# A decoder trunk on one core: the down weights' sums behind the units' stores, the down product's parts made further ahead and spread

## The chip, the core and the metric

The kernel runs on one core of a Trainium2 chip. The metric is the device time of one execution in microseconds (us), the median of several runs. The engines are named as in the profile: PE is TensorE (matmuls), PEld its weight loads, DVE is VectorE, ACT is ScalarE, POOL is GpSimd and SP is SyncE, which here only issues DMAs. Each engine takes its instructions in the order in which they stand in its own queue. The framework's planner draws up these orders when the kernel is built, from the order of the program, from priorities that the program sets, from the dependences between tiles, and from edges that the program adds.

## The reference

One layer of a decoder on 1024 tokens of width 1024, all in float32. An attention sub-layer with three groups of heads comes first, then the part that matters here, a gated MLP with D_FF = 2816, then a gated embedding and a last norm:

```
r = r + mix @ w_out
h2 = rmsnorm(r, ffn_norm)
gate = causal_dwconv(h2 @ w_gate) + conv_b
r = r + (gelu(gate) * (h2 @ w_up)) @ w_down
gate = sigmoid(rmsnorm(r, ple_norm) @ w_ple_gate)
r = r + (p @ w_ple_proj) * gate
return rmsnorm(r, final_norm)
```

## The kernel before

Every float32 matmul is made of three: each operand is split into a high part, rounded to the matmul's type (ACT, line 770), and a low part, the rest (DVE, line 771), and `mm3` (lines 113 to 117) adds high by high, high by low and low by high in PSUM.

**The output projection** (`out_tile_half`, lines 810 to 819) makes r tile by tile, in 16 halves. Each takes a slice of w_out, loaded by SP and split by ACT (line 102) and DVE (line 104), and a half of the residual's input; the result is also stored to HBM by POOL (`r_dram`, line 818).

**The units.** The MLP's 22 tiles of 128 hidden channels are 22 units. Gate and up product of one unit are computed together by seven products of half size (a Strassen scheme: sums of weights and sums of activations are multiplied instead of the four blocks). A product (`prod`, line 916) is 12 matmuls of 128x512, a unit 84. The products add into three PSUM banks "a", "b" and "d"; between them ACT copies a bank out (line 941) or DVE adds it to a tile (lines 944 and 978), and the product that adds into the same bank next has to wait for that. The order from unit 3 on is 1, 5, 6, 2, 7, 3, 4, with the addition of line 944 between 7 and 4 (while 3 runs). The weights of a unit are prepared one to two units ahead (`weights_up_1`, `weights_up_2`, with a high priority). At its end a unit multiplies by the gate (lines 988 and 989) and POOL stores the result for the down product: an even unit stores `he` (line 992), an odd one `ho`, then the differences with its even partner, `ta` and `tb` (lines 995, 1000 and 1003).

**The sums of the down weights** (`sums_down`, lines 1005 to 1015). The down product is of the same scheme, so it needs sums of the blocks of w_down. They are made in 22 slices: POOL loads four blocks of 128x256 (512 KB, line 1009) into one tile for which there is a single buffer (tag "rs"), DVE makes four additions (lines 1011 and 878), POOL stores the tile to HBM (`s_dram`, line 1015). They depend on no unit. In the program slice n stands before unit n+3, but the planner gives them the place where the engines' queues are free for them: POOL issues the first load at 385.2 us, in the attention's end, and the last at 733.4 us, in the middle of the units.

**The down product** (lines 1062 to 1164) has seven products in the order `DOWN = (1, 2, 6, 5, 7, 3, 4)`, each of 11 steps (one for each pair of units), 77 steps in all. A step is 12 matmuls. Its operands are 512 KB of weights and activations for two steps, loaded from HBM by SP and split by ACT and DVE, a pair of steps at a time (`parts`, lines 1073 to 1089): weights into the buffers "whi" and "wlo" (two each), activations, loaded for four steps, into "big" (16). Raw weights go to "wraw" (one buffer) and "ws" (three), raw activations to "hx" (six). At step 4 all eight tiles of the residual are loaded back (`residual`, line 1097), which fills four of the six "hx" buffers. At the end of a product DVE adds its four banks to the residual (line 1156), and where a quarter of the residual is then complete (`DONE`) the program makes at once, for its four tiles, the squares for the next norm and the high and low part that the gate's matmuls will read (`done`, lines 1105 to 1121). After the products 2, 6 and 5 a slice of the gate's weights is prepared (`gate_weights`).

**The gate and the end** (`embed`, `finish`) follow, 24 groups of 24 matmuls.

Of the kernel before, what the change touches and what calls it, by code (L numbers as in the profile page):

```python
# [73 lines left out]
def trunk(ctx: ExitStack, tc: tile.TileContext, a, out, dbg):  # L74
# [18 lines left out]
    def half(h):  # L93
        return slice(h * H2, (h + 1) * H2)
# [696 lines left out]

    he_dram = [dp.tile([P, H2], F32, name=f"hed{j}") for j in range(NJ)]
    ho_dram = [dp.tile([P, T], F32, name=f"hod{j}") for j in range(NJ)]
    ta_dram = [dp.tile([P, T], F32, name=f"tad{j}") for j in range(NJ)]
    tb_dram = [dp.tile([P, T], F32, name=f"tbd{j}") for j in range(NJ)]
    s_dram = [dp.tile([4, P, H2], F32, name=f"sd{j}") for j in range(NJ)]
    B = {n: [None] * 4 for n in range(1, 8)}
# [111 lines left out]
    class Unit:  # L909
# [21 lines left out]
        def rest(self):  # L931
# [59 lines left out]
            if f % 2 == 0:  # L991
                G.dma_start(he_dram[j], u1)
# [9 lines left out]
            minus(e1, u1, t2)  # L1002
            G.dma_start(tb_dram[j], even[j])

    def sums_down(n):

        j, c = n // 2, slice(n % 2 * 256, n % 2 * 256 + 256)
        t = cp.tile([P, 4, 256], F32, tag="rs", bufs=1, name=f"sd{n}")
        G.dma_start(t, a["w_dn"][j][:, :, c].rearrange("b p c -> p b c"))
        a11, a12, a21, a22 = [t[:, i, :] for i in range(4)]  # L1010
        V.tensor_tensor(out=a22, in0=a21, in1=a22, op=ALU.add)
        minus(a21, a11, a21)
        minus(a11, a22, a11)
        minus(a12, a12, a11)
        G.dma_start(s_dram[j][:, :, c].rearrange("b p c -> p b c"), t)

    even = []
    lft = [t[:, half(0)] for t in r]
# [45 lines left out]

    def operands(i, j):

        w = a["w_dn"][j]
        x = {1: w[0], 2: w[1], 4: w[3], 6: s_dram[j][0], 3: s_dram[j][1], 7: s_dram[j][2], 5: s_dram[j][3]}[i]
        y = {1: he_dram[j], 2: ho_dram[j][:, half(1)], 3: ho_dram[j][:, half(0)], 5: ta_dram[j][:, half(0)],
             6: ta_dram[j][:, half(1)], 7: tb_dram[j][:, half(0)], 4: tb_dram[j][:, half(1)]}[i]  # L1070
        return x, y

    def parts(g):

        with tc.high_priority(offset=300):
            if g % 2 == 0:
                raws[g // 2] = f4("hx", f"hr{g}", (P, 4, H2))
                for x in range(4 * (g // 2), min(len(steps), 4 * (g // 2) + 4)):
                    nc.sync.dma_start(raws[g // 2][:, x % 4, :], operands(*steps[x])[1])
            n = min(2, len(steps) - 2 * g)  # L1080
            rw = f4("ws" if g % 2 else "wraw", f"wdr{g}", (P, 2, H2))
            for x in range(n):
                nc.sync.dma_start(rw[:, x, :], operands(*steps[2 * g + x])[0])
            got = []
            for raw, tags in ((rw, ("whi", "wlo")), (raws[g // 2][:, g % 2 * 2:g % 2 * 2 + 2, :], ("big", "big"))):
                hi, lo = [f4(t, f"{c}{t}d{g}", (P, 2, H2), F32R) for c, t in zip("hl", tags)]
                hl(hi[:, :n], lo[:, :n], raw[:, :n])
                got.append((hi, lo))
        return got
# [15 lines left out]
    def done(d, h):  # L1105

        c = half(h)
        if not acc3:
            acc3.append(f4("ws", "acc3"))
        if d == (0 if h else 4):  # L1110
            S.square(acc3[0][:, c], r[d][:, c])
        else:
            sq = fp.tile([P, H2], F32, tag="s1", bufs=1, name=f"sq{d}{h}")
            S.square(sq, r[d][:, c])
            V.tensor_tensor(out=acc3[0][:, c], in0=acc3[0][:, c], in1=sq, op=ALU.add)
# [4 lines left out]
        V.scalar_tensor_tensor(out=lo[:, c], in0=r[d][:, c], scalar=col(C_G3 + d), in1=hi[:, c].bitcast(F32),  # L1120
                               op0=ALU.mult, op1=ALU.subtract)
# [15 lines left out]
    got = {}  # L1137
    bank = {}
    for n, (i, j) in enumerate(steps):
        if n % 2 == 0:  # L1140
            got[n // 2] = parts(n // 2)
        if n == 4:
            for x in range(4):
                residual(x)
        (wh, wl), (xh, xl) = got[n // 2]
# [7 lines left out]
        if j == NJ - 1:  # L1153
# [147 lines left out]
def layout(x, p, positions, attn_norm, w_in, hgrn_lb, hgrn_gnorm, attn_sinks, w_out, ffn_norm, w_gate, w_up, conv_w,  # L1301
# [15 lines left out]
    }  # L1317
    a["w_dn"] = w_down[0].reshape(NJ, 2, P, 2, H2).transpose(0, 3, 1, 2, 4).reshape(NJ, 4, P, H2)
    a.update(constants())
# [18 lines left out]
```

## Time and profile before

| | us |
|---|---|
| median of 3 runs | 1305.1 |
| lowest and highest | 1305.02, 1309.39 |
| the profiled execution's own time | 1310.03 |
| its span, first to last instruction | 1308.3 |
| output projection and embedding's first product, about | 404 to 531 |
| units | 531 to 972 |
| down product | 972 to 1197 |
| gate, embedding, last norm | 1197 to 1308 |

| engine | busy us | share |
|---|---|---|
| PE | 1249.9 | 96% |
| DVE | 907.7 | 69% |
| ACT | 553.1 | 42% |
| POOL | 128.1 | 10% |

The mean granted clock of TensorE in this execution is 0.982 of full speed. Views of the trace that are used below: the page (shares of each engine), the view by stretches (busy time, instruction counts and clock in given windows), the timeline (instructions of one engine in order, with the idle time before each and what ended it), the view of waits (who waited for whom) and the table of DMA issues (size, and median time from issue to landing). "sd<-w_dn" is a load of a slice of the down weights, "sd<-sd" its store; "wdr", "hr" and "rr" are raw weights, raw activations and the residual of the down product.

### The profile page before, as it was taken

The numbers are of one execution on the slowest core, as the hardware profiler recorded it, in microseconds if no ns is written. First come the engines' busy times: TensorE is split into PE (matmuls) and PEld (weight loads), VectorE is DVE, ScalarE is ACT, GpSimd is POOL, SyncE is SP. The second block draws the span as 40 slices with busy tenths as digits, with TensorE's granted clock in tenths as the row PEclk, the third lists the DMA queues.
The fourth block names the chain that finished last, engine by engine and source line by source line (L and its number), as shares of the span: only waits on it lengthen the run. The fifth ranks groups of instructions, "written<-read, shape, count | busy, mean of one in ns | idle before, by whom it ended". The sixth has DMA issues, their size and how long they took to land. (4 is left out here: it accounts for less than half of the span.)

```text
span 1308.3 us, 16434 instructions
## 1 busy us (share of the span) xinstructions
PE 1249.9 (96%) x6198; PEld 1041.7 (80%) x6198; DVE 907.7 (69%) x1567; ACT 553.1 (42%) x860; POOL 128.1 (10%) x162
## 2 busy tenths in 40 slices
PE   9999999999999789999999999999999899899996
PEld 7888888887888577777777788888887788688896
DVE  7986967566776377988777766776666555565576
ACT  6324233356773143644334343433344433453432
POOL 2000000021112223011112100000000000000010
PEclk9999999999999889999999999999999899899998
DMA  6110011111017746354555423332568555443132
GB/s 245 49 33 24 26 33 33 33 33 33 17 49 256 252 159 217 113 166 172 185 191 184 153 77 105 121 110 94 167 238 295 182 190 170 135 161 116 41 106 81
DMA packets 62414, 165.04 MB, mean 126 GB/s; under 512 B 7488, under 2 KB 10048, under 8 KB 62336
## 3 DMA queue, kind: packets, MB, share of 16 engines
q1 hardware_dynamic: 45136, 106.45, 24.7%
q0 software_dynamic: 15616, 55.84, 12.0%
q10 hardware_dynamic: 1584, 1.71, 0.4%
q8 instruction: 48, 0.79, 0.2%
q14 instruction: 30, 0.25, 0.1%
HBM read 119.67 MB, written 44.30 MB: 125 GB/s over the span
## 5 line engine op out<-in xcount | busy, mean ns | idle before, releaser
L115 PE MATMUL d<-hbigd,hwhid 128*128 128x512 f32 x308 | 122.2, 398 | 6.8 <-ACT hwhid L770 4.2
L116 PE MATMUL d<-lbigd,hwhid 128*128 128x512 f32 x308 | 122.1, 397 | 1.2 <-DVE lbigd L771 1.2
L117 PE MATMUL d<-hbigd,lwlod 128*128 128x512 f32 x308 | 121.8, 395 | 0.7 <-DVE lwlod L771 0.7
L771 DVE TENSOR_TENSOR lwlod<-wdr,hwhid 128x1024 fp32r<-128x1024 f32 (+1 forms) x39 | 47.0, 1208 | 70.8 <-ACT hwhid L770 70.7
L770 ACT CAST hwhid<-wdr 128x1024 fp32r<-128x1024 f32 (+1 forms) x39 | 40.4, 1039 | 99.6 <-PE d L116 98.0
L115 PE MATMUL gb<-b,hf 128*128 128x512 f32 x176 | 70.2, 399 | 6.5 <-DVE us L944 4.8
L115 PEld LDWEIGHTS d<-hbigd,hwhid 128*128 128x128 f32 x308 | 59.0, 192 | 20.5 <-ACT hwhid L770 5.0
L115 PE MATMUL gd<-b,f 128*128 128x512 f32 x176 | 68.9, 392 | 3.5 <-ACT us L941 3.4
L116 PEld LDWEIGHTS d<-lbigd,hwhid 128*128 128x128 f32 x308 | 59.1, 192 | 14.2 <-DVE lbigd L771 1.9
L117 PEld LDWEIGHTS d<-hbigd,lwlod 128*128 128x128 f32 x308 | 59.1, 192 | 13.7 <-DVE lwlod L771 1.5
L117 PE MATMUL gd<-b,f 128*128 128x512 f32 x176 | 68.3, 390 | 1.5 <-DVE f L771 1.5
L116 PE MATMUL gb<-b,hf 128*128 128x512 f32 x176 | 69.3, 394 | 0.0
L117 PE MATMUL gb<-b,lf 128*128 128x512 f32 x176 | 69.3, 394 | 0.0
L116 PE MATMUL gd<-b,f 128*128 128x512 f32 x176 | 68.5, 389 | 0.0
L115 PE MATMUL pg<-hp,hpg 128*128 128x256 f32 (+1 forms) x192 | 61.7, 321 | 0.0
L116 PE MATMUL pg<-lp,hpg 128*128 128x256 f32 (+1 forms) x192 | 61.3, 319 | 0.0
L117 PE MATMUL pg<-hp,lpg 128*128 128x256 f32 (+1 forms) x192 | 61.1, 318 | 0.0
L771 DVE TENSOR_TENSOR lbigd<-hr,hbigd 128x1024 fp32r<-128x1024 f32 (+1 forms) x39 | 46.9, 1206 | 11.7 <-ACT hbigd L770 11.4
L770 ACT CAST f<-wg 128x512 fp32r<-128x512 f32 x22 | 13.7, 624 | 80.2 <-PE gd L117 80.2
L115 PEld LDWEIGHTS gb<-b,hf 128*128 128x128 f32 x176 | 33.3, 189 | 17.9 <-DVE us L944 6.9
L770 ACT CAST hbigd<-hr 128x1024 fp32r<-128x1024 f32 (+1 forms) x39 | 40.3, 1038 | 16.3 <-DMA hr<-hod 8.9
L771 DVE TENSOR_TENSOR f<-s,f 128x1024 fp32r<-128x1024 f32 x22 | 26.9, 1222 | 28.0 <-ACT f L770 27.8
(459 smaller groups left out, 3513.1 us busy)
## 6 DMA issues: line engine op xcount, KB each, us to landing
sd<-w_dn POOLq DMA_DIRECT2D x22, 512.0 KB, 4.3
sd<-sd POOLq DMA_DIRECT2D x22, 512.0 KB, 3.8
wu<-w_gu SPq DMA_DIRECT2D x22, 512.0 KB, 3.5
wg<-w_gu SPq DMA_DIRECT2D x22, 512.0 KB, 3.6
wdr<-sd SPq DMA_DIRECT2D x44, 256.0 KB, 3.0
wdr<-w_dn SPq DMA_DIRECT2D x33, 256.0 KB, 3.0
wr_wo<-w_out SPq DMA_DIRECT2D x16, 512.0 KB, 4.0
hod<-us POOLq DMA_DIRECT2D x11, 512.0 KB, 3.1
```

Of the source, the lines that this page charges most:

```text
L115: TE.matmul(o, wh, xh, start=first, stop=False, skip_group_check=on)
L116: TE.matmul(o, wh, xl, start=False, stop=False, skip_group_check=on)
L117: TE.matmul(o, wl, xh, start=False, stop=last, skip_group_check=on)
L770: S.copy(hi, src)
L771: e.tensor_tensor(out=lo, in0=src, in1=hi.bitcast(F32), op=ALU.subtract)
```

## The change

1. `sums_down(n)` queues its load behind the last store of unit n+2 (unit 21 for the last three) with an edge in POOL's queue (`issue_after`). Each unit notes its last store in `sent`. In an odd unit the `ho` store moves behind the `ta` store.
2. The buffers in HBM for `he`, `ho`, `ta`, `tb` and the sums become one tensor each over all pairs, with w_down laid out to match, so that the loads of up to four steps become one DMA (`load_steps`).
3. The down product's weights are split into "r" buffers (eight, which is four pairs of steps) from pair 2 to pair 32, and into "whi" and "wlo" or "big" before and after; raw weights rotate over "wraw" and two turns of "ws".
4. The residual's tiles are loaded at the steps 4, 6, 12 and 15, two tiles each, instead of all at step 4.
5. `done` is no longer called for four tiles at once: the calls go to a list, and one is taken at every odd j (the step within a product), from step 56 on at every step. For the first four tiles the parts are made once at full width, when the second half is complete.

```diff
-    he_dram = [dp.tile([P, H2], F32, name=f"hed{j}") for j in range(NJ)]
...
-    s_dram = [dp.tile([4, P, H2], F32, name=f"sd{j}") for j in range(NJ)]
+    he_dram = dp.tile([NJ, P, H2], F32, name="hed")
+    ho_dram, ta_dram, tb_dram = [dp.tile([NJ, P, T], F32, name=n) for n in ("hod", "tad", "tbd")]
+    s_dram = dp.tile([4, NJ, P, H2], F32, name="sd")
...
-                G.dma_start(he_dram[j], u1)
+                sent[f] = G.dma_start(he_dram[j], u1)
...
-            G.dma_start(ho_dram[j], us)
...
             G.dma_start(ta_dram[j], cv)
...
-            G.dma_start(tb_dram[j], even[j])
+            G.dma_start(ho_dram[j], us)
+            sent[f] = G.dma_start(tb_dram[j], even[j])
...
-        G.dma_start(t, a["w_dn"][j][:, :, c].rearrange("b p c -> p b c"))
+        with tc.issue_after(sent[min(n + 2, NF - 1)].ins):
+            G.dma_start(t, a["w_dn"][:, j, :, c].rearrange("b p c -> p b c"))
...
+    def load_steps(t, x0, n, which):
+
+        x = x0
+        while x < x0 + n:
+            i, j = steps[x]
+            m = min(x0 + n - x, NJ - j)
+            nc.sync.dma_start(t[:, x - x0:x - x0 + m, :], OPERANDS[i][which][j:j + m].rearrange("j p t -> p j t"))
+            x += m
+
+    LAST = 6 * NJ // 2
...
-                for x in range(4 * (g // 2), min(len(steps), 4 * (g // 2) + 4)):
-                    nc.sync.dma_start(raws[g // 2][:, x % 4, :], operands(*steps[x])[1])
+                load_steps(raws[g // 2], 2 * g, min(4, len(steps) - 2 * g), 1)
             n = min(2, len(steps) - 2 * g)
-            rw = f4("ws" if g % 2 else "wraw", f"wdr{g}", (P, 2, H2))
-            for x in range(n):
-                nc.sync.dma_start(rw[:, x, :], operands(*steps[2 * g + x])[0])
+            rw = f4(("wraw", "ws", "ws")[g % 3], f"wdr{g}", (P, 2, H2))
+            load_steps(rw, 2 * g, n, 0)
+            tags = ("whi", "wlo") if g < 2 or g >= LAST and (g - LAST) % 3 else ("r", "r") if g < LAST else ("big", "big")
...
+        if d < 4:
+            if h:
+                return
+            c = slice(0, T)
...
+    todo = []
     for n, (i, j) in enumerate(steps):
         if n % 2 == 0:
             got[n // 2] = parts(n // 2)
-        if n == 4:
-            for x in range(4):
-                residual(x)
+        if n in (4, 6, 12, 15):
+            residual((4, 6, 12, 15).index(n))
+        if n > 5 * NJ and todo or todo and j % 2:
+            done(*todo.pop(0))
...
             if i in DONE:
-                d0, h = DONE[i]
-                for d in range(4):
-                    done(d0 + d, h)
+                todo += [(DONE[i][0] + d, DONE[i][1]) for d in range(4)]
...
+    for x in todo:
+        done(*x)
```

More of the change, by code (lines that the diff above doesn't have):

```diff
@@ L1014, in sums_down @@
         minus(a12, a12, a11)
-        G.dma_start(s_dram[j][:, :, c].rearrange("b p c -> p b c"), t)
-    even = []
+        G.dma_start(s_dram[:, j, :, c].rearrange("b p c -> p b c"), t)
+    even, sent = [], {}
     lft = [t[:, half(0)] for t in r]
@@ L1063, in trunk @@
     raws = {}
[L1065 to L1071, printed above, removed]
+    wd = a["w_dn"]
+    OPERANDS = {1: (wd[0], he_dram), 2: (wd[1], ho_dram[:, :, half(1)]), 4: (wd[3], tb_dram[:, :, half(1)]),
+                6: (s_dram[0], ta_dram[:, :, half(1)]), 3: (s_dram[1], ho_dram[:, :, half(0)]),
+                7: (s_dram[2], tb_dram[:, :, half(0)]), 5: (s_dram[3], ta_dram[:, :, half(0)])}
+    def load_steps(t, x0, n, which):
[6 more added lines that the diff above has]
+    LAST = 6 * NJ // 2
     def parts(g):
@@ L1077, in parts @@
                 raws[g // 2] = f4("hx", f"hr{g}", (P, 4, H2))
[L1078 to L1079 removed]
+                load_steps(raws[g // 2], 2 * g, min(4, len(steps) - 2 * g), 1)
             n = min(2, len(steps) - 2 * g)
[L1081 to L1083 removed]
+            rw = f4(("wraw", "ws", "ws")[g % 3], f"wdr{g}", (P, 2, H2))
+            load_steps(rw, 2 * g, n, 0)
+            tags = ("whi", "wlo") if g < 2 or g >= LAST and (g - LAST) % 3 else ("r", "r") if g < LAST else ("big", "big")
             got = []
[L1085 to L1086 removed]
+            for raw, ts in ((rw, tags), (raws[g // 2][:, g % 2 * 2:g % 2 * 2 + 2, :], ("big", "big"))):
+                hi, lo = [f4(t, f"{c}{'wh'[len(got)]}d{g}", (P, 2, H2), F32R) for c, t in zip("hl", ts)]
                 hl(hi[:, :n], lo[:, :n], raw[:, :n])
@@ L1317, in layout @@
     }
-    a["w_dn"] = w_down[0].reshape(NJ, 2, P, 2, H2).transpose(0, 3, 1, 2, 4).reshape(NJ, 4, P, H2)
+    a["w_dn"] = w_down[0].reshape(NJ, 2, P, 2, H2).transpose(3, 1, 0, 2, 4).reshape(4, NJ, P, H2)
     a.update(constants())
```

3 lines of the change are left out of this document (removed).

## The prediction

> **What bounds the kernel now.** The page comes first, for the engine that the span hangs on.
>
> ```profile
> span 1308.3 us, 16434 instructions
> PE 1249.9 (96%) x6198; PEld 1041.7 (80%) x6198; DVE 907.7 (69%) x1567; ACT 553.1 (42%) x860; POOL 128.1 (10%) x162
> ```
>
> TensorE (PE) is busy 96% of the span. What can be won without taking matmuls away is PE's idle time, and time at a lowered clock. The view by stretches shows where these lie: its columns are the stretch, its length, the busy time and instruction count of PE, PEld, DVE, ACT and POOL, the granted clock, the DMA engines' busy share and GB/s.
>
> ```profile
> 404.00:424.00 20.00, 18.76 (x82) 14.91 (x81) 9.88 (x14) 6.52 (x8) 6.57 (x9) 1.00 0.98 350
> 424.00:446.00 22.00, 15.53 (x56) 12.24 (x55) 6.17 (x10) 4.35 (x6) 6.98 (x8) 0.77 0.80 273
> 446.00:456.00 10.00, 8.33 (x38) 6.55 (x37) 4.87 (x8) 2.25 (x4) 2.53 (x4) 1.00 0.60 197
> 456.00:476.00 20.00, 15.35 (x66) 12.64 (x65) 12.45 (x31) 5.11 (x7) 4.81 (x7) 0.83 0.69 223
> ...
> 531.00:572.00 41.00, 36.49 (x156) 28.54 (x155) 36.80 (x56) 21.14 (x30) 2.23 (x3) 1.00 0.37 125
> 572.00:745.00 173.00, 162.93 (x696) 130.45 (x695) 137.59 (x201) 66.43 (x80) 28.22 (x42) 0.99 0.51 174
> 745.00:965.00 220.00, 219.96 (x971) 181.88 (x970) 152.48 (x188) 87.06 (x105) 12.90 (x24) 1.00 0.34 115
> ...
> 985.00:995.00 10.00, 8.76 (x38) 6.63 (x37) 6.41 (x6) 6.00 (x6) 0.00 (x0) 1.00 0.83 276
> ...
> 1030.00:1046.00 16.00, 12.35 (x43) 9.40 (x42) 11.36 (x15) 7.59 (x11) 0.00 (x0) 0.79 0.50 165
> ...
> 1130.00:1146.00 16.00, 12.15 (x42) 9.01 (x41) 12.45 (x16) 9.37 (x14) 0.00 (x0) 0.79 0.47 154
> ```
>
> The stretch 745:965 is undisturbed: 971 matmuls in 220 us, 0.2266 us each. With that as the price of one, a stretch loses its length less its count times 0.2266. (Counts include matmuls that straddle an end, and a few of 128 columns, so this is good to some 0.3 us.) In the order of the rows: 20 - 82 x 0.2266 = 1.4; 9.3; 1.4; 5.0; 5.7; 15.3; nothing; 1.4; 6.3; 6.5. So 17.1 us go in the output projection (404 to 476), 21.0 in the first half of the units (531 to 745) and 14.2 in the down product. These 52 us are what the change can reach. The second half of the units runs without loss, with the same code.
>
> What differs between the halves of the units is the sums of the down weights. The timeline of DVE shows what they do to it, in the projection and in the units; the bracket is the idle time before an instruction and what ended it.
>
> ```profile
> 435.31 0.42 DVE L1011 TENSOR_TENSOR sd<-sd 128x256 f32<-128x256 f32 x1 [10.02 <-DMA sd<-w_dn]
> ...
> 451.07 0.43 DVE L1011 TENSOR_TENSOR sd<-sd 128x256 f32<-128x256 f32 x1 [5.22 <-DMA sd<-w_dn]
> ...
> 464.56 0.43 DVE L1011 TENSOR_TENSOR sd<-sd 128x256 f32<-128x256 f32 x1 [5.60 <-DMA sd<-w_dn]
> ...
> 737.35 0.42 DVE L1011 TENSOR_TENSOR sd<-sd 128x256 f32<-128x256 f32 x1 [2.81 <-DMA sd<-w_dn]
> ...
> 738.30 0.68 DVE L944 TENSOR_TENSOR us<-gb,us 128x512 f32<-128x512 f32 x1
> ```
>
> DVE takes its instructions in order. At L1011, the first sum of a slice, it stands still until the slice has landed, and all that is queued behind it stands as well: the weights' low parts at L104 in the projection, in the units L944, which empties the bank that PE's next product adds to. The timeline of PE answers within 2 us:
>
> ```profile
> 436.92 0.80 PE L117 MATMUL o<-ha,wl_wo 128*128 128x512 f32 x1 [6.47 <-DVE wl_wo L104]
> ...
> 739.04 0.50 PE L115 MATMUL gb<-b,hf 128*128 128x512 f32 x1 [1.91 <-DVE us L944]
> ...
> 1037.77 0.79 PE L115 MATMUL d<-hbigd,hwhid 128*128 128x512 f32 x1 [3.65 <-ACT hwhid L770]
> ...
> 1136.09 1.22 PE L115 MATMUL d<-hbigd,hwhid 128*128 128x512 f32 x2 [2.66 <-ACT hbigd L770]
> ```
>
> The last two are the down product's own stalls. The DVE rows just before the second show the cause: the residual's additions (L1156) and the gate's parts and squares (L1120, L1115) come in one bunch after a product's last step, and the next steps' weights and operands (L771) stand among and behind them.
>
> ```profile
> 1130.44 1.88 DVE L1156 TENSOR_TENSOR rr<-d,rr 128x512 f32<-128x512 f32 x3
> 1132.24 0.74 DVE L1120 SCALAR_TENSOR_TENSOR lp<-rr,small,hp 128x512 fp32r<-128x512 f32 x1
> 1132.90 0.68 DVE L1115 TENSOR_TENSOR acc<-acc,sq 128x512 f32<-128x512 f32 x1
> 1133.50 1.41 DVE L1120 SCALAR_TENSOR_TENSOR lp<-rr,small,hp 128x512 fp32r<-128x512 f32 x2
> 1134.83 1.22 DVE L771 TENSOR_TENSOR lwlod<-wdr,hwhid 128x1024 fp32r<-128x1024 f32 x1
> ```
>
> **The sums leave the projection.** Nothing is removed: 22 loads and 22 stores on POOL's queue and 88 additions on DVE remain, at 0.42 us about 37 us of DVE. They move. The edge puts load n behind the last store of unit n+2, so no sum can start before unit 2 is done, three units of 19 us (84 matmuls) after 531. In the projection the three long blocks of DVE go, and with them 9.3 + 1.4 + 5.0 = 15.7 us of PE. What is late next are the loads of w_out and of the residual: with the DMA engines 98% busy the stretch from 404 lost 1.4 us, so I leave as much standing and take 14.3. Bounds: 5, if these loads take over two thirds of it, and 16.5, if the sums' traffic was also what made them late.
>
> **The sums in the units.** 13 of them lie in 531 to 745 now, at a loss of 15.3 us from 572 on: 1.2 us per sum. The 5.7 us before 572 belong to the first units (the operands' parts, and a weight load on which ACT waits) and stay. After the change 19 sums lie in the units, one to each of 19, always at the same place in the unit. Whether that place is harmless I work out in an undisturbed unit.
>
> ```profile
> 751.17 0.53 POOL L1003 DMA_DIRECT2D tbd<-us  x1 [0.41 <-DVE us L878]
> ...
> 768.50 0.55 POOL L992 DMA_DIRECT2D hed<-us  x1 [16.80 <-DVE us L989]
> ```
>
> ```profile
> 752.94 1.22 DVE L771 TENSOR_TENSOR f<-s,f 128x1024 fp32r<-128x1024 f32 x1 [2.07 <-ACT f L770]
> ...
> 757.30 0.68 DVE L944 TENSOR_TENSOR us<-gb,us 128x512 f32<-128x512 f32 x1
> ```
>
> ```profile
> 759.82 0.39 PE L115 MATMUL gb<-b,hf 128*128 128x512 f32 x1
> ```
>
> ```profile
> sd<-w_dn POOLq DMA_DIRECT2D x22, 512.0 KB, 4.3
> ...
> wdr<-sd SPq DMA_DIRECT2D x44, 256.0 KB, 3.0
> ...
> hr<-hod SPq DMA_DIRECT2D x22, 256.0 KB, 5.6
> ...
> rr<-rd SPq DMA_DIRECT2D x8, 512.0 KB, 7.1
> ```
>
> After an odd unit the load is issued at 751.7, when the tbd store has left POOL, and lands 4.3 us later, at 756.0. The matmul that needs L944 starts at 759.82. If the planner puts L1011 right behind the low part of 752.94, DVE waits from 754.2 to 756.0, then has 1.7 us of sums and, up to the end of L944, 3.2 us of its own work: 760.9, so PE waits 1.1 us. If it stands two instructions later, it delays nothing that PE waits for: L944 ends at 757.98 + 1.7 = 759.7. After an even unit the load is issued at 769.05 and lands at 773.35, and the same sum (4.9 us) gives 778.3; PE's matmul is due 84 matmuls after 759.82, at 778.86: no wait. With half of the 1.1 us in 9 odd units that is 5 us; the loss of 15.3 becomes 5, a gain of 10.3. Bounds: 0 per sum (gain 15.3), or the 1.2 per sum of now, 22.8 in all (7.5 worse than now). DVE has room: it was idle 67 of the 220 us from 745 on, and 19 sums put 32 us there and before.
>
> Moving the ho store behind the ta store delays it by about 2 us (it waits for the second subtraction); who waits is ACT's next copy into a "us" buffer at L941, needed by PE's product 3, which begins some 3 us later. POOL's queue has nothing else behind these loads. I cost it at nothing; if the cover is gone, it is at most 1 us in an odd unit.
>
> **The down product.** The gate's parts of a row tile come one or two steps apart, and the weights' parts are made into "r" buffers, four pairs ahead where "whi" and "wlo" allow two. A pair is 24 matmuls, 5.4 us, so the lead grows from 11 to 22 us, and the bunch, four tiles of 0.6 + 0.7 + 0.7 us on DVE, is under 10. The stalls of 6.3 and 6.5 us go; for the four tiles whose parts are now made at full width from step 66 on I leave 0.8 us: gain 12.0, between 8 and 12.8. The larger loads (up to four steps in one) move the same bytes with fewer issues on SP; they cost nothing while the lead holds.
>
> What gets worse is the start of the product. The last three sums stand behind unit 21's last store, which now leaves POOL at about 980, one after another through one buffer. There the DMA engines are 83 to 100% busy, the residual tiles take 7.1 us to land, and the lead is only what was made before 972. A load in such company blocked DVE for 10.02 us at 425. On the other side the residual's four loads are spread over twelve steps, and the weights' lead fills faster. From 0 to 10 us more than the 1.4 of now; I take 2, near the lower end, since the pairs' parts go before the sums in the planner's order. The stores' buffers in HBM become one each for he, ho, ta, tb and the sums. Should a load now wait for all stores to its buffer, the sums' last store (980 plus three rounds of 13 us, the 173 us of the stretch over its 13 sums: 1019) still lies ahead of step 22, at 1030. The rest, from 1197 on, is not touched.
>
> **Sum.** 14.3 + 10.3 + 12.0 - 2 = 34.6 us. The profiled execution took 1310.0 us (1308.3 and 1.7 around it), which gives 1275.4. The median of the runs shown is 4.9 lower, 1305.1, and I take the gain over to it: 1270.5.
>
> **Rivals.** *The sums cost in every unit what they cost now*, 1.2 us. For it is the row of the view of waits for 572 to 745 (us in total, times, longest), by which six of 13 sums made DVE wait, at no fixed place:
>
> ```profile
> DVE sd L1011 <- DMA sd<-w_dn: 16.3, 6, 4.1
> ```
>
> Against it is the fixed place worked out above. Then 14.3 - 7.5 + 12.0 - 2 = 16.8: 1288. *Loads take over*: PE in the projection and at the start of the product then waits for DMA. For it are the shares of 0.98 and 0.80; against it that they include the sums' own traffic. 5 + 10.3 + 8 - 10 = 13.3: 1292. *The change doesn't do what it says*: the edge binds POOL alone, the planner fills DVE's queue anew, and blocks of the same length arise elsewhere; the projection's 14.3 come back as waits in the units, and in the down product one of two stalls stays (12.0 - 6.3) while its start costs 5: under 1 us, 1304. *Slower*: every sum hits L944 as the one at 737 did. PE waited 1.91 us there and then ran cold, 3.4 us in all (the row below); 19 of these are 65 against 14.3 + 15.3 + 12.0 - 2 = 39.6, so 1305.1 + 25 = 1330. It decides from 2.1 us per sum. Against it: only one of 13 sums did so.
>
> The cold clock is the other part of that price:
>
> ```profile
> 736.00:746.00 10.00, 8.09 (x29) 6.16 (x29) 7.77 (x12) 3.97 (x4) 0.75 (x1) 0.83 0.40 128
> ```
>
> 10 - 29 x 0.2266 = 3.4, though PE waited only 1.91. The Trainium skill (TensorE: Matmul & The Clock Gate, "HAM oscillation — how this bites in real kernels") has the clock fall after idle gaps of more than about 3.4 us. By that rule the slower rival would cost the wait alone, 19 x 1.91 = 36 against 39.6, and would end at 1302. The row disagrees: 1.91 us were enough here, so I keep 1330.
>
> **Chances.** The forecast has 0.68, sums as dear as now 0.13, loads 0.09, no change 0.05, slower 0.05. The range reaches from 1257 (all best bounds give 16.5 + 15.3 + 12.8 = 44.6, 1260.5, and a little for the stall of 5.7 that I left) to 1290, past the first rival, and leaves out the others. About 0.5% (6.5 us) is what a measurement of this kernel can tell from no change. Faster by more: the first three cases but for their tails, 0.88; the same 0.07; slower 0.05.
>
> **What would show it.** Right: no L1011 before the third unit is done; PE at 46 matmuls per 10 us from 415 to 510; 22 units at 19.0 to 19.6 us each; no clock below 1.00 near 1035 and 1140; the first sum of each unit waiting under 2 us. Wrong: L944 or L104 still releasing PE after a wait for sd; PE waits on hbigd or hwhid between 975 and 1030 of over 4 us in all; a unit pitch over 20.

## The result

| | before | after |
|---|---|---|
| median of 4 runs each, us | 1305.06 | 1272.21 |
| lowest and highest | 1303.04, 1309.39 | 1269.89, 1273.43 |
| ratio, with its 95% interval | | 0.9742 (0.9713 to 0.977) |
| the profiled execution, its span | 1310.03, 1308.3 | 1272.79, 1270.8 |

The forecast was 1270.5. The page of the changed kernel shows PE's busy share up by a point on a span 37.5 us shorter:

```profile
span 1270.8 us, 16249 instructions
PE 1236.2 (97%) x6198; PEld 1034.7 (81%) x6198; DVE 903.2 (71%) x1563; ACT 551.7 (43%) x856; POOL 130.2 (10%) x162
```

The view by stretches, with the columns explained in the prediction, for the projection (first four rows), the units (three) and the down product (two):

```profile
404.00:424.00 20.00, 20.00 (x89) 16.38 (x88) 8.52 (x10) 7.74 (x10) 6.75 (x8) 1.00 0.92 322
424.00:446.00 22.00, 22.00 (x103) 18.36 (x102) 9.18 (x12) 6.65 (x9) 5.81 (x7) 1.00 0.77 281
446.00:456.00 10.00, 10.00 (x50) 8.37 (x49) 7.28 (x20) 3.54 (x6) 2.49 (x3) 1.00 0.49 147
456.00:476.00 20.00, 20.00 (x90) 16.58 (x89) 17.22 (x22) 11.35 (x15) 8.35 (x8) 1.00 0.39 127
508.00:549.00 41.00, 35.94 (x149) 28.39 (x148) 33.64 (x49) 19.63 (x29) 0.72 (x1) 0.96 0.29 98
549.00:722.00 173.00, 170.94 (x746) 139.06 (x745) 137.19 (x190) 71.78 (x87) 22.23 (x35) 1.00 0.47 153
722.00:944.00 222.00, 218.57 (x960) 179.36 (x958) 167.97 (x233) 87.83 (x104) 28.87 (x44) 1.00 0.53 174
1015.00:1025.00 10.00, 6.99 (x24) 5.04 (x23) 7.68 (x8) 6.88 (x8) 0.00 (x0) 0.83 0.53 176
1025.00:1159.00 134.00, 134.00 (x593) 110.99 (x592) 75.60 (x79) 56.38 (x64) 1.43 (x2) 1.00 0.53 176
```

PE is busy in all 72 us of the projection that lost 17.1 before, and in all 134 us from 1025 to 1159, at a clock of 1.00. Counted by matmuls, the second old stall stood ahead of the 57th step, which PE now starts at 1102.32, inside these 134 us; the first stood ahead of the 23rd, which it now starts at 1004.07, and there it lost 0.7 us (at 1005.22). Two things are new: a hole of 10 - 24 x 0.2266 = 4.6 us at 1015, and small losses all along the units (549 to 944), whose second half had none before.

From here on a stage's length runs from its first matmul to that of the next stage. What PE lost in it is the time between the starts of two matmuls beyond the price of the first, summed over the timeline of PE.

| stage | before: length, lost | after: length, lost | gain by the loss | forecast |
|---|---|---|---|---|
| projection, 395 to the units | -, 23.6 | -, 0.7 | 22.9 | 14.3 |
| units | 440.6, 21.7 | 435.7, 16.7 | 5.0 | 10.3 |
| down product | 225.0, 15.6 | 215.2, 5.7 | 9.9 | 12.0 - 2 |
| gate and end | 110.9 | 111.3 | -0.4 | 0 |

Three terms, each off by something, add up to 37.4 against a forecast of 34.6; by the medians the gain is 32.9. The profiled execution of before lay 5 us above its median, that of after 0.6, so the table's losses before are those of a long execution.

The timeline of DVE shows where the sums stand now; the bracket is the idle time before an instruction and what ended it:

```profile
664.69 0.42 DVE L1010 TENSOR_TENSOR sd<-sd 128x256 f32<-128x256 f32 x1 [1.75 <-DMA sd<-w_dn]
...
669.10 0.69 DVE L942 TENSOR_TENSOR us<-gb,us 128x512 f32<-128x512 f32 x1
...
840.15 0.68 DVE L942 TENSOR_TENSOR us<-gb,us 128x512 f32<-128x512 f32 x1
...
841.35 0.42 DVE L1010 TENSOR_TENSOR sd<-sd 128x256 f32<-128x256 f32 x1
...
919.05 0.42 DVE L1010 TENSOR_TENSOR sd<-sd 128x256 f32<-128x256 f32 x1 [3.12 <-DMA sd<-w_dn]
...
984.56 0.42 DVE L1010 TENSOR_TENSOR sd<-sd 128x256 f32<-128x256 f32 x1 [10.15 <-DMA sd<-w_dn]
...
1001.21 0.42 DVE L1010 TENSOR_TENSOR sd<-sd 128x256 f32<-128x256 f32 x1 [6.01 <-DMA sd<-w_dn]
```

The place in the unit isn't one: at 841 the sum stands behind L942 and waits for nothing, at 664 and 919 ahead of it, and PE then waited 1.08 us at 669.84 and 1.34 us at 920.59. From 643 to 905 it changes with the unit: a slice that was loaded behind an odd unit's store has its sum behind L942, one behind an even unit's store some 4 us ahead of it. The view of waits for 549 to 944 counts these (us in total, times, longest):

```profile
DVE sd L1010 <- DMA sd<-w_dn: 17.4, 12, 3.6
...
PE gb L115 <- DVE us L942: 4.5, 4, 1.4
```

The hole at 1015 is a chain, in the view of it: the last sum waits for its load; the low parts behind it come late; so a raw buffer comes free late, the next weights are issued at 1008.6, take 8.3 us, and PE stands.

```profile
993.09 8.00 DMA sd<-w_dn
...
1001.21 0.42 DVE sd L1010
...
1006.21 1.22 DVE lwd L771
...
1008.59 0.36 SPq L1075
...
1009.00 8.31 DMA wdr<-sd
...
1017.33 1.05 ACT hwd L770
...
1018.41 1.24 DVE lwd L771
...
1019.69 0.79 PE d L117
```

### The profile page after: what moved, and what is told of

Read it like the earlier page. It is cut to its first block, busy times and chain, and to the rows that moved or that the text cites. A ratio compares the mean times of both kernels' runs of the same rounds, so it can differ in the third digit from the quotient of the medians.

```text
span 1270.8 us, 16249 instructions
## 1 busy us (share of the span) xinstructions
PE 1236.2 (97%) x6198; PEld 1034.7 (81%) x6198; DVE 903.2 (71%) x1563; ACT 551.7 (43%) x856; POOL 130.2 (10%) x162
## 5 line engine op out<-in xcount | busy, mean ns | idle before, releaser
L115 PE MATMUL d<-hhd,hwd 128*128 128x512 f32 x308 | 120.5, 391 | 2.5 <-ACT hwd L770 2.5
L117 PE MATMUL d<-hhd,lwd 128*128 128x512 f32 x308 | 120.8, 392 | 1.1 <-DVE lwd L771 1.1
L116 PE MATMUL d<-lhd,hwd 128*128 128x512 f32 x308 | 120.4, 391 | 0.0
L771 DVE TENSOR_TENSOR lwd<-wdr,hwd 128x1024 fp32r<-128x1024 f32 (+1 forms) x39 | 47.0, 1209 | 44.0 <-ACT hwd L770 43.9
L770 ACT CAST hwd<-wdr 128x1024 fp32r<-128x1024 f32 (+1 forms) x39 | 40.3, 1038 | 78.7 <-PE d L116 63.5
L115 PEld LDWEIGHTS d<-hhd,hwd 128*128 128x128 f32 x308 | 58.2, 189 | 14.9 <-ACT hwd L770 2.9
L117 PEld LDWEIGHTS d<-hhd,lwd 128*128 128x128 f32 x308 | 58.2, 189 | 13.9 <-DVE lwd L771 1.9
L116 PEld LDWEIGHTS d<-lhd,hwd 128*128 128x128 f32 x308 | 58.1, 189 | 12.1
L770 ACT CAST hhd<-hr 128x1024 fp32r<-128x1024 f32 (+1 forms) x39 | 39.8, 1035 | 33.5 <-DMA hr<-tad 17.9
L771 DVE TENSOR_TENSOR lhd<-hr,hhd 128x1024 fp32r<-128x1024 f32 (+1 forms) x39 | 46.5, 1206 | 8.0 <-ACT hhd L770 7.8
L770 ACT CAST f<-wg 128x512 fp32r<-128x512 f32 x22 | 13.7, 623 | 84.0 <-PE gd L117 84.0
```

The costliest lines, as they stand in the source:

```text
L115: TE.matmul(o, wh, xh, start=first, stop=False, skip_group_check=on)
L116: TE.matmul(o, wh, xl, start=False, stop=False, skip_group_check=on)
L117: TE.matmul(o, wl, xh, start=False, stop=last, skip_group_check=on)
L770: S.copy(hi, src)
L771: e.tensor_tensor(out=lo, in0=src, in1=hi.bitcast(F32), op=ALU.subtract)
```

## The experiments

The theory after the result: the sums cost wherever DVE stands at one of their loads ahead of work that PE needs; the edge moves that out of the projection; the longer lead and the spread of the gate's parts take the two stalls of the down product. Twelve kernels; the kernel before took 1303.2 to 1304.4 beside them.

| kernel | median | ratio to before (95%) | units | down | lost: projection, units, down |
|---|---|---|---|---|---|
| e1 traffic in the projection | 1284.2 | 0.984 (0.9818 to 0.9863) | 433.8 | 209.9 | 16.0, 14.9, 0.7 |
| e2 without the edge | 1292.1 | 0.9911 (0.9882 to 0.994) | 439.1 | 209.4 | 20.0, 20.2, 0.0 |
| e3 the edge alone | 1294.2 | 0.9918 (0.9897 to 0.994) | 434.6 | 238.3 | 0.7, 15.6, 28.8 |
| e4 sums three units earlier | 1271.9 | 0.9746 (0.9723 to 0.9768) | 439.8 | 209.5 | 0.5, 20.9, 0.2 |
| e5 sums in the middle | 1271.3 | 0.9754 (0.9729 to 0.978) | 440.9 | 209.4 | 0.6, 21.9, 0.0 |
| e6 copies in the projection | 1313.3 | 1.008 (1.0052 to 1.0108) | 435.1 | 209.5 | 45.6, 16.2, 0.1 |
| e7 no sums | 1260.5 | 0.9676 (0.9647 to 0.9705) | 428.3 | 209.4 | 0.6, 9.4, 0.0 |
| e8 no edge, lead of two pairs | 1292.0 | 0.9913 (0.9879 to 0.9946) | 439.9 | 209.4 | 20.6, 21.0, 0.0 |
| e9 the additions' places set | 1267.2 | 0.9724 (0.9704 to 0.9743) | 434.2 | 210.7 | 0.5, 15.3, 1.2 |
| e10 no edge, bunches | 1304.0 | 0.9998 (0.9975 to 1.0021) | 439.9 | 220.8 | 18.5, 21.0, 11.3 |
| e11 no edge, both undone | 1302.2 | 0.9986 (0.9969 to 1.0003) | 439.7 | 219.1 | 20.9, 20.8, 9.6 |
| e12 places set, two pairs | 1271.0 | 0.975 (0.9736 to 0.9764) | 427.4 | 220.8 | 0.6, 8.5, 11.4 |

**e1, the sums' traffic back in the projection**, with nobody on DVE waiting for it.

```diff
+    idle_dram = dp.tile([P, 4, 256], F32, name="idled")
+    for n in range(9):
+        t = cp.tile([P, 4, 256], F32, tag="rs", bufs=1, name=f"idl{n}")
+        G.dma_start(t, a["w_dn"][:, n, :, :256].rearrange("b p c -> p b c"))
+        G.dma_start(idle_dram, t)
```

> The changed kernel with nine loads and nine stores of 512 KB added in the output projection, through the sums' single buffer and on POOL's queue, as the first nine sums were, but with no addition on DVE behind them (they copy data that nobody reads). Theory, DVE's queue stood behind the slices: the projection keeps its speed, since nothing on an engine waits for these loads; 1272 to 1276 us, and no wait of PE for L104 over 2 us. Rival, the sums' traffic made w_out and the residual late: the projection loses again 10 us or more of its 23; 1282 to 1290 us.

The time lies in the rival's range, but not for its reason. The timeline of PE, then the view of waits for 400 to 470:

```profile
457.61 1.84 PE L150 MATMUL ss_r<-ones,acc 128*128 128x1 f32 x8 [9.88 <-issue]
```

```profile
POOL idled L843 <- DMA idl<-w_dn: 27.7, 6, 8.1
...
DVE acc L779 <- POOL acc L779: 13.1, 1, 13.1
```

One stall of 13.7 us makes nearly all of the loss. The row of PE names no releaser; what its matmul reads is the sum of squares, which DVE completed at 457.51 after its 13.1 us of waiting for POOL. POOL, which takes its instructions in order, stood at the added stores until their loads had landed, and the squares of the norm, which POOL adds up (L779), stood behind it. Up to that place PE lost 1.8 us, where the kernel before lost 11.8 up to 447. From 424 to 446, where the kernel before lost 9.3, it lost nothing, with the DMA engines busy 94%:

```profile
424.00:446.00 22.00, 22.00 (x99) 18.22 (x98) 5.75 (x6) 5.54 (x8) 7.62 (x9) 1.00 0.94 338
```

The 1.8 are nearly all one wait, at 414.81, for a late load of the residual's input (DVE of the kernel before, of e1 and of the changed kernel, in this order):

```profile
412.56 1.34 DVE L817 TENSOR_TENSOR r<-o,r 128x512 f32<-128x512 f32 x2 [2.89 <-DMA r<-xT]
...
413.97 1.34 DVE L815 TENSOR_TENSOR r<-o,r 128x512 f32<-128x512 f32 x2 [2.95 <-DMA r<-xT]
...
410.91 1.32 DVE L815 TENSOR_TENSOR r<-o,r 128x512 f32<-128x512 f32 x2 [1.51 <-DMA r<-xT]
```

Behind them PE waited 1.10 us, 1.58 us and not at all. So the traffic by itself costs some 2 us, through this load, and the wait, moved from DVE's queue to POOL's, costs 13.7.

**e6, traffic without any wait**: two copies within HBM behind each of the first nine stores of the result.

```diff
+        put = G.dma_start(r_dram[d][:, c], r[d][:, c])
+        for x in range(2 if 8 * h + d < 9 else 0):
+            with tc.issue_after(put.ins):
+                G.dma_start(spare[2 * (8 * h + d) + x], a["w_dn"][x::2, d])
```

> The changed kernel with 18 copies of 512 KB within HBM added in the output projection, two behind each of the first nine stores of the result on POOL. Nobody reads or waits for them; they add DMA load but no wait in POOL's queue. Theory after the first traffic run (there the squares' additions on POOL stood behind POOL's waits for the added loads, and the load on the DMA engines itself cost only some 2 us): 1272 to 1276, no stall near 457 to 465. Rival (the DMA engines' load in the projection makes w_out and the residual late): 1282 or more, with PE waiting for the weights' parts in the projection.

Missed, and of little use: the planner drew up another order. POOL's first addition of the squares waited 60 us for ACT and came at 490, and several stalls of 10 us follow from that; besides, w_out did come late (PE lost 5.9 us at 448). It shows that 18 unthrottled copies hurt, not what the sums' traffic does.

**e2, everything but the edge.**

```diff
-        with tc.issue_after(sent[min(n + 2, NF - 1)].ins):
-            G.dma_start(t, a["w_dn"][:, j, :, c].rearrange("b p c -> p b c"))
+        G.dma_start(t, a["w_dn"][:, j, :, c].rearrange("b p c -> p b c"))
```

> The changed kernel without the edge: the sums go where the planner puts them; everything else stays. Theory, the edge brings what the projection and the units gained (22.8 and 5.3 us in the profiles) and the down product's parts the rest: the projection and the units are as before, the down product gains some 14 (its start has no sums): 1289 to 1293 us. Rival, the fewer and larger loads and the new buffers bring part of the projection's and units' gain: below 1284 us.

As expected: the projection loses 20.0 again, the units 20.2, the down product nothing. The edge is worth some 20 us, and the 5.7 lost between 1005 and 1023 are its price.

**e3, the edge alone** on the kernel before: the `issue_after` of part 1 of the diff, with `sent` and the moved `ho` store.

> The kernel before with the edge and the moved ho store alone. Theory: projection and units as in the changed kernel (minus 28 us), the down product with both of its stalls (13 us) and the cost of three sums at its start (4 us): 1279 to 1283 us. Rival, the down product's stalls were not the bunch and the two pairs of lead but late sums (the loads of sd that ended at 1035): they shrink here too, 1270 to 1275 us.

Missed by 11 us. Projection and units are those of the changed kernel, but the down product takes 238.3. The timeline of PE in it:

```profile
983.58 0.80 PE L117 MATMUL d<-hbigd,lwlod 128*128 128x512 f32 x1 [5.03 <-DVE lwlod L771]
...
996.78 0.79 PE L117 MATMUL d<-hbigd,lwlod 128*128 128x512 f32 x1 [4.74 <-DVE lwlod L771]
```

DVE waited 7.23 and 7.58 us for slices just before (at 979.99 and 994.03). With weights only two pairs ahead PE stands each time, 8.0 and 6.4 us; in the changed kernel waits of 10.15 and 6.01 us cost 5.7 in all. The old stalls (5.6 at 1023, 6.3 at 1120) are there as well. So the edge creates a wait which another part of the change has to cover; which part, e8 to e12 tell.

**e8, e10, e11: lead and spread apart**, on e2, where no late sum disturbs.

```diff
-            tags = ("whi", "wlo") if g < 2 or g >= LAST and (g - LAST) % 3 else ("r", "r") if g < LAST else ("big", "big")
+            tags = ("whi", "wlo")
```

> The run without the edge (1292.1, down product 209.4 with no loss), with the weights' parts back at two pairs ahead: whi and wlo for all pairs. The spread of the gate's parts and of the residual's loads stays. Theory (a bunch of DVE work longer than the lead makes the two stalls, so either part alone takes most of them): 1292 to 1294, down product within 2 us of 209.4. Rival (the longer lead is what takes them): 1302 to 1306, down product 220 or more, PE waiting at 1020 to 1040 and 1120 to 1140.

```diff
-        if n > 5 * NJ and todo or todo and j % 2:
-            done(*todo.pop(0))
...
-                todo += [(DONE[i][0] + d, DONE[i][1]) for d in range(4)]
+                for d in range(4):
+                    done(DONE[i][0] + d, DONE[i][1])
```

> The run without the edge (1292.1; down product 209.4, no loss; with two pairs of lead also 209.4) with the gate's parts in bunches of four again; the four pairs of lead stay. Theory (either part alone takes the two stalls of the kernel before): 1292 to 1295, down product 209 to 212. Rival (the spread is what takes them, the lead does nothing): 1302 to 1306, down product 220 to 224, PE waiting near 1035 and 1140.

e11 has both edits.

> The run without the edge with both undone: two pairs of lead and bunches of four. The residual's loads stay spread and the loads of several steps stay joined. Theory: both stalls of the kernel before are back, down product 221 to 224, 1303 to 1306. Rival (the spread residual loads or the joined loads were what took them): 209 to 212, 1292 to 1295.

The stretch from 1126 to 1136 of e2, e10 and e11, in this order:

```profile
1126.00:1136.00 10.00, 10.00 (x46) 8.27 (x45) 6.39 (x7) 5.05 (x5) 0.00 (x0) 1.00 0.65 241
```

```profile
1126.00:1136.00 10.00, 6.46 (x20) 4.88 (x21) 9.36 (x11) 6.32 (x8) 0.00 (x0) 0.83 0.45 142
```

```profile
1126.00:1136.00 10.00, 5.89 (x18) 4.46 (x19) 8.79 (x10) 5.84 (x7) 0.00 (x0) 0.83 0.37 121
```

My theory held for e8 and e11 (e11's 1302.2 and 219.1 lie just below the ranges named), and fell for e10: with the spread alone no stall is left; with the lead alone both are there, as large as with neither. For the second stall the timelines of DVE and PE of e10 tell why:

```profile
1127.74 0.68 DVE L1120 TENSOR_TENSOR acc<-acc,sq 128x512 f32<-128x512 f32 x1
1128.34 0.74 DVE L1129 SCALAR_TENSOR_TENSOR lp<-rr,small,hp 128x512 fp32r<-128x512 f32 x1
1129.00 1.22 DVE L771 TENSOR_TENSOR lhd<-hr,hhd 128x1024 fp32r<-128x1024 f32 x1
```

```profile
1127.86 0.73 PE L115 MATMUL d<-hhd,hwd 128*128 128x512 f32 x2 [2.66 <-ACT hhd L770]
1130.27 0.59 PE L116 MATMUL d<-lhd,hwd 128*128 128x512 f32 x1 [1.67 <-DVE lhd L771]
```

PE waits for hhd and lhd, the parts of the *activations*. The lead was lengthened for the weights; the activations' parts of the next step still stood in the bunch (L1120, L1129). At the first stall it is otherwise. The timelines of PE and ACT of e10 there:

```profile
1030.82 0.50 PE L115 MATMUL d<-hhd,hwd 128*128 128x512 f32 x1 [2.98 <-ACT hwd L770]
```

```profile
1029.20 0.63 ACT L1119 ACTIVATE sq<-rr 128x512 f32<-128x512 f32 x1 [0.39 <-DVE acc L1120]
1029.74 1.03 ACT L770 CAST hwd<-wdr 128x1024 fp32r<-128x1024 f32 x1
```

PE waits for hwd, a part of the *weights*, which have the buffers for a lead of four pairs. These raw weights were loaded at 1019.52, behind a load of activations in SP's queue, and landed at 1025.45; then ACT had squares of the norm (L1119) and a part of the gate's weights before them in its own queue. In e2 the same pair's high part was made at 1011.98, 16 us before PE used it. So the buffers were there, and the queues' orders did not use them at this place; why the planner chose these orders isn't shown.

**e4 and e5, the sums behind other units.** e4 makes each slice three units earlier, behind unit n-1 (its calls in the program move too); e5 begins behind unit 2, makes two slices in four of the units and the last behind unit 19.

```diff
-        with tc.issue_after(sent[min(n + 2, NF - 1)].ins):
+        with tc.issue_after(sent[max(n - 1, 0)].ins):
```

> The changed kernel with every sum three units earlier: slice n behind the store of unit n-1 (the first two behind unit 0's), so that none is left after unit 21. Theory, what the down product still loses at its start (5.7 us in the profile) comes from DVE standing 10.2 and 6.0 us at the last sums: it falls to 1 or 2, total 1267 to 1269 us. Rival, it is the DMA engines' load there (residual tiles, four pairs of parts): the loss stays, 1271 to 1273 us; or the first units pay for their sums: above 1273 us.

```diff
-        with tc.issue_after(sent[min(n + 2, NF - 1)].ins):
+        with tc.issue_after(sent[BEHIND[n]].ins):
...
+    BEHIND = (2, 3, 4, 5, 6, 7, 7, 8, 9, 9, 10, 11, 11, 12, 13, 13, 14, 15, 16, 17, 18, 19)
```

> The changed kernel with the sums behind other units: the first behind unit 2, then one per unit, two behind each of the odd units 7, 9, 11 and 13, the last behind unit 19, so that none is left for units 20 and 21 or the start of the down product. Theory (a sum is harmless in a steady unit and dear only where the down product's own loads and parts are on the way): units at most 436 us, down product 209.5 as in the run without the edge, together about 6 us less than the changed kernel, 1265 to 1268. Rival (every sum has a price wherever it stands, so that moving them changes nothing, as with all sums two units earlier): 1271 to 1274, with the units at 440 or more. A second one: two sums in a unit block DVE twice for the one buffer; then losses of over 1 us in units 8, 10, 12 and 14.

Both took the hole from the down product, as expected, and lost as much in the units: 1271.9 and 1271.3, no different from 1272.2. So both totals missed the theory's, and e5's rival gave its number. In e4 one stall at 946 (PE waited 3.22 us) is not a sum's; e9 below shows the same one. In e5 one stall of 6.2 us does most of it: behind a pair of slices the next one had to wait for the one buffer and was loaded only at 745.36, and DVE stood 3.01 us at it, up to 749.24, ahead of the gate's addition; the convolution and ACT's activation came late, and PE:

```profile
757.30 0.80 PE L115 MATMUL gb<-b,f 128*128 128x512 f32 x1 [3.15 <-ACT s L939]
```

Where the load is tied to is not enough: the planner still chooses where the addition stands.

**e7, no sums at all**: loads, additions and stores left out, plain blocks of w_down read in their place.

```diff
-        sums_down(f - 3)
...
-                6: (s_dram[0], ta_dram[:, :, half(1)]), 3: (s_dram[1], ho_dram[:, :, half(0)]),
+                6: (wd[0], ta_dram[:, :, half(1)]), 3: (wd[1], ho_dram[:, :, half(0)]),
```

> The changed kernel without the sums of the down weights: no load, addition or store of them, and the down product reads plain blocks of w_dn in their place, so the output differs by that. It gives what all 22 sums still cost. Theory (the stalls of 7.7 us in units 3 to 21 and of 5.7 at the start of the down product are theirs): 1258 to 1262, units about 428 to 430, down product 209.5. Rival (those stalls have other causes, as a late load of the units' weights or the pairs' parts): 1266 or more, with losses left in units 3 to 21 or at the start of the down product.

1260.5: the 22 sums still cost 11.7 us in the changed kernel, by the losses 16.7 - 9.4 = 7.3 in the units and 5.7 in the down product. Their 37 us of additions and 22 MB of traffic are hidden but for that. Of the 9.4 left, 7.2 lie in the first units.

**e9, the additions tied to a place as well**, in DVE's queue:

```diff
+    def sums_add(got, behind):
...
+        with tc.issue_after(behind.ins):
+            V.tensor_tensor(out=a22, in0=a21, in1=a22, op=ALU.add)
...
-                plus(u1, "b")
+                self.mark = plus(u1, "b")
...
-        sums_down(f - 3)
-        Unit(f, A).rest()
+        got = sums_load(f - 3)
+        unit = Unit(f, A)
+        unit.rest()
+        sums_add(got, unit.mark)
...
+            if n // 2 in (6, 8, 10):
+                sums_add(load, lows[n // 2])
```

> The changed kernel with the loads of the sums where they are, and an edge in DVE's queue as well: the first addition of slice n stands behind the addition of the bank (L942, between the products 7 and 4) of unit n+3, 6 to 8 us after its load was issued; those of the last three slices stand behind the low parts of the pairs 6, 8 and 10 of the down product. Traffic and additions are the same. Theory (what the sums still cost is DVE standing at a load that has not landed, in front of work that PE waits for; the run without sums took 1260.5): units 428 to 432, down product 209 to 211, 1261 to 1265. Rival (the cost is the additions' own time on DVE or their traffic): units still 434 or more, or a loss at the start of the down product, 1269 to 1273.

1267.2, between theory and rival, and the stretches say where:

```profile
549.00:938.00 389.00, 385.83 (x1696) 317.33 (x1694) 303.13 (x415) 158.85 (x189) 50.33 (x78) 1.00 0.49 165
938.00:945.00 7.00, 5.09 (x16) 4.09 (x17) 6.04 (x10) 3.41 (x4) 0.75 (x1) 0.76 0.91 342
```

From 552 to 938 PE now loses 1.2 us with all the traffic and all the additions in place, so the theory held there. One stall of 6.4 remains, and it isn't a sum's. The timelines of ACT and of DVE at its place:

```profile
935.82 1.99 ACT L770 CAST hhd<-hr 128x1024 fp32r<-128x1024 f32 x2 [5.13 <-DMA hr<-hed]
```

```profile
936.89 2.36 DVE L771 TENSOR_TENSOR lhd<-hr,hhd 128x1024 fp32r<-128x1024 f32 x2 [4.95 <-ACT hhd L770]
939.17 0.68 DVE L942 TENSOR_TENSOR us<-gb,us 128x512 f32<-128x512 f32 x1
```

The down product's first activations were loaded late and stood ahead of L942: the same mechanism with another load. e4 had the same stall at 946.

**e12, that stall removed, and the lead taken away under late sums.** Edits of e9: the tags of e8, and

```diff
+                if g in (2, 3) and raw is not rw:
+                    with tc.issue_after(unit.gate.ins):
+                        lows[g] = hl(hi[:, :n], lo[:, :n], raw[:, :n])
```

> The run with the additions' places set (1267.2), with two edits that show in different stages. First, in the end of the units: there the low parts of the down product's pairs 2 and 3 stood before L942 of unit 21 and waited for their activations (a loss of 6.4 us); they now stand behind the addition of the gate's bank in unit 21. Theory: units 427 to 429 instead of 434.2. Rival (another wait takes the place): 432 or more. Second, in the down product: the weights' parts are two pairs ahead as in the kernel before; the spread stays. If the lead does nothing (as in the runs without the edge): down product 209 to 211.5, the whole 1259 to 1263. If the loads of the last sums need the longer lead at the product's start: down product 214 or more, PE waiting for the weights' parts between 938 and 1020, the whole 1265 or more.

The units take 427.4, less than without sums in e7. In the down product the rival's case came: 220.8 instead of 210.7. The timelines of DVE and PE:

```profile
979.59 0.42 DVE L1016 TENSOR_TENSOR sd<-sd 128x256 f32<-128x256 f32 x1 [9.59 <-DMA sd<-w_dn]
```

```profile
982.79 0.80 PE L117 MATMUL d<-hhd,lwd 128*128 128x512 f32 x1 [5.78 <-DVE lwd L771]
```

DVE stood at a slice for 9.59 us; the high parts it needed next were there from 976 on (ACT had itself waited up to 973.9, for the gate's weights), and PE lost 8.6 us. In e9, with four pairs of lead, DVE stood as long at the same sum, and its whole down product lost 1.2:

```profile
982.41 0.43 DVE L1016 TENSOR_TENSOR sd<-sd 128x256 f32<-128x256 f32 x1 [8.54 <-DMA sd<-w_dn]
```

That is what the lead is for. (The changed kernel itself with two pairs was not run; e12 against e9 is the nearest.) e12's units with e9's down product would give a span of 1267.9 - 10.1 = 1257.8; this kernel was not run, so it is an estimate. Of those run, e9 is the fastest that computes the sums; its interval and the changed kernel's overlap.

## Why the prediction was right, step by step

**Total and sign** were right, with compensating errors in the terms: the projection gave 8.6 us more than forecast, units and down product together 5.4 less. That the median came within 2 us of the forecast is in part luck.

**The projection** (14.3 forecast, 22.9 measured). The mechanism was right: DVE's blocks went, and PE with them. Mis-sized was the term, twice. I counted 17.1 us in four stretches; by the timeline of PE the kernel before lost 23.6, among them 7.2 (not 5.0) at 469, where the norm's factors stood behind a sum, and 3.2 at 509 in front of the norm's squares, outside the four stretches. And of the 1.4 us left standing for late loads none stayed: at a DMA share of 0.92 the stretch from 404 lost nothing. The loss there before was a late load indeed (PE's 1.1 us at 413.40 were released by DVE's L817, which had waited 2.89 us for the residual's input), but it was the sums' traffic that made it late, since PE has the same wait in e1 and none there in the changed kernel. That is the condition which I had given to the upper bound only.

**The units** (10.3 forecast, 5.0 measured). Worked out from one odd and one even unit, the price of a sum was 0 to 1.1; it came out at 7.3 / 19 = 0.4 on average, inside that, down from 1.2. But "always at the same place in the unit" failed: the sum stands ahead of L942 at 664 and 919, behind it at 841. And the working had the units the wrong way round: it gave the odd ones up to 1.1 us and the even ones none, but the sums behind odd units went behind L942, and three of PE's four waits on it (669.84, 746.96, 941.37) follow even units. That the average fits is therefore luck. The loads, 5.1 us from issue to landing by the median of 549 to 944 instead of 4.3, added to it. The first units, which I left at 5.7, lost 7.6, with or without sums (7.2 in e7): ACT's and DVE's bunch of operands and a late weight load, which the change doesn't touch. Of the 6.0 us by which the units lost more than the 10.7 that the forecast left, 1.9 are the first units', 1.9 the sums', and 2.2 are there without sums too (e7). The pitch was 435.7 / 22 = 19.8, just over the 19.6 that I named; the first sum came at 598.80, behind unit 2, as named.

**The stalls of the down product** (12.0 forecast; of these stalls nothing is left). The size was about right: the down product lost 15.6 in the profiled execution of before, but 9.6 in e11, which has the same two stalls, and by the medians the spread is worth 10 to 12. The reason was half wrong. I let lead and bunch work together ("the lead grows from 11 to 22 us and the bunch is under 10"). e8, e10 and e11 show that the spread alone takes the stalls and the lead none of them. At the second stall the row that I had quoted said so: PE waited on hbigd there, an activation's part, and the lead was given to the weights. At the first the row named hwhid, a weight's part, and e10 waits for the same part with twice the buffers: more buffers were not more lead, since load and split stood late in the queues of SP and ACT.

**The start of the down product** (2 forecast, 5.7 measured, 0 to 10 in the range). The cause was the one named, the last sums waiting beside a busy DMA; what I missed is that it hits late, through a raw buffer, at 1018. Here the lead earns its place: without it the late sums cost 9 to 14 us (e12, e3).

**The rivals.** "Sums as dear as now" fell (0.4 each), "loads take over" fell, "slower" fell: PE waited on L942 only 4 times, 1.4 us at most (and at 941.37 low parts of the down product stand between the sum and L942 as well). Two of the signs did speak against the forecast: L942 (then L944) still released PE after a wait for sd, and the first sum of a unit waited up to 3.6 us where under 2 was named. "No change" came close in one respect: blocks do arise elsewhere in DVE's queue, 13 us of them by e7, and moving the sums (e4, e5) only moves them.

By part: the edge alone 9 (e3 against before, medians), the spread 10 to 12 (e8 and e2 against e11 and e10, medians), the lead 10 (the down products of e9 and e12, one profile each), together 30 to 31 of the 32.9. These were taken on different kernels, so that they add up is not shown. The rest of the change, which e11 has, is worth some 2 by the medians, and between nothing and 4 by the interval (0.9969 to 1.0003). Without the edge the lead is worth nothing (e8 against e2), since what it covers is made by the edge.

## What to carry to other kernels

An edge on a load fixes when it is issued, not where its consumer stands; on an engine that takes its instructions in order, tie the consumer too, behind the work that must not wait, and far enough behind the load that it has landed. When several parts of a change aim at one stall, look which operand the waiting instruction names: a lead on another one doesn't help. And count a lead from the time at which load and split are done, not in buffers: the queues may not use them. When work moves, count what the stage it leaves loses instruction by instruction, since stretches chosen by eye miss the small stalls.

## What the runs showed of the hardware

A wait of PE has two prices. At 669.84 and 920.59 the waits of 1.08 and 1.34 us cost just themselves: behind them the matmuls soon start 0.23 us apart. Behind the waits of 2.49 and 0.53 us at 1018 and 1019 the view of the chain has them 0.43 us apart, and the stretch's clock is 0.83. The Trainium skill (TensorE: Matmul & The Clock Gate, "HAM oscillation — how this bites in real kernels") lets the clock fall after gaps of more than about 3.4 us. This case shows it after 2.49, as before after 1.91. The length of the wait doesn't decide it alone: a wait of 2.48 us at 540.43 in the kernel before left the clock at 1.00 (536 to 546), and of two waits of 2.98 us, at 1030.82 in e10 and at 1032.98 in e11, only the first has the lower clock in its stretch (the rows of e10 and e11):

```profile
1028.00:1038.00 10.00, 7.18 (x24) 5.75 (x25) 8.04 (x9) 5.98 (x8) 0.00 (x0) 0.83 0.42 132
```

```profile
1028.00:1038.00 10.00, 7.02 (x31) 5.47 (x30) 7.94 (x10) 5.25 (x7) 0.00 (x0) 1.00 0.38 127
```

That is 4.6 and 3.0 us lost for the same wait; what decides it stays open. The loads of the slices (512 KB) land in 5.1 us by the median in the units; at the start of the down product one took 8.0 us and one of raw weights of the same size 8.3, at a DMA share of 0.85 and 0.88 meanwhile: an order that works in one stage has 3 us less margin in another.
